# GLU contraction in two parts around the S5 steps of a hybrid decoder trunk, and a chunk's gelu and split one step behind its state

## The chip, the cores and the metric

The kernel runs on one core of one Trainium2 chip. The metric is the device time of one execution in microseconds; the time before is 2535.65 us, the median of three runs (2535.18 to 2535.86). A TensorE clock of 1.0 in the tables is 2.4 GHz, 0.5 is 1.2 GHz.

## The reference

One inference step of a trunk with two layers, each followed by a SwiGLU feed-forward network (FFN) with 5632 hidden channels. The first layer is an even one (retention beside a gated recurrence, after one projection), the second an odd one:

```
u = rmsnorm(x, g)
h_t = A h_{t-1} + B u_t          # S5: 128 groups of 16 channels, 64 complex states each
y_t = Re(C h_t) + d * u_t
y = gelu(y)
z = y @ w_glu + b_glu            # 2048 x 4096
z1, z2 = split(z, 2)
x = x + z1 * sigmoid(z2)
x = x + swiglu(rmsnorm(x, g2))
```

The tokens are a prompt of 256 and 8 samples of 4; the kernel holds them as 288 columns, 72 (8 samples and 64 chunks of the prompt) for each of 4 positions. All is float32.

## The kernel before

**Matmuls.** A product in float32 is made of three in a shorter type: a high part of the weights (`wh`) times the high and the low part of the operand, and the low part (`wl`) times the high part (lines 314 to 316). A *unit* makes one output tile of 128 channels; one *k* is 128 input channels, so 3 matmuls of 288 columns. GLU has 16 k and 32 units, z and g for each of 16 output tiles.

**Weights.** They come in *slots* of half a unit, 8 k for GLU. For each slot SyncE loads `raw` (line 262, 4 buffers), ScalarE copies it to `wh` (line 268, 4 buffers), and VectorE subtracts to get `wl` (line 274, through the helper at L96). The `wl` buffers are a list, `ring`: three, and a fourth, `wlx`, that `to_ffn0` adds for all that follows the first layer's mixer. A buffer returns to the free list when the last matmul of its slot has been issued in program order; the next `wl` takes the oldest free one.

**Order.** All engines' queues are written out by hand in one pass of `run_prog` over a list of items (a unit's half, or a function). Ahead of every item, a function too, the loop at lines 294 to 303 loads and splits ahead of the slots used up:

```
while c[1] < min(c[0], done + LH + 1, n):
    prep_next()
if c[2] >= done + (4 if hold else 3) or c[2] >= n or c[2] in hold:
    break
prepl_next()
```

So `wl` is kept three slots ahead; while `hold` is set (the S5 steps but the last), four, and not the slot named in it.

**S5.** `s5_open` (in the background queue near the end of FFN0) opens the buffers and loads the first tables. `s5_core` computes the norm and then runs 16 steps, one for each chunk of 128 channels (8 groups). `stage_a(j)` issues loads of tables P, R, T and O for the next steps, then P of chunk j+1 (`st_a`: a VectorE multiply by the norm, then 32 narrow matmuls into `pp`, L1396), the first half of chunk j's recurrence on VectorE (`st_b1`: two products, a sum), and T of chunk j (`st_t`: 32 narrow matmuls into `po`, L1446). `stage_b(j)` issues O of chunk j-1 (`st_o`: 64 narrow matmuls that need the state `Hs` of chunk j-1, L1456) and the second half of chunk j (`st_b2`: two scans, two products, and their difference, the state `Hs`). Gelu and split of a chunk follow two to four steps behind: `st_d1` (three ScalarE operations), `st_d1b` (a product, tanh), `st_d2` (VectorE, ScalarE), `st_d3` (VectorE).

**GLU beside S5.** Between `stage_a(t)` and `stage_b(t)`, from t = 4, stand the matmuls of one k, t-4, of the first two units, over the full 16 k; four more stages after the steps (t = 16 to 19) end them, and a third unit runs in a bank of its own. The other 29 units follow, each over all 16 k at once.

Of the kernel before, what the change touches and what calls it, by code (L numbers as in the profile page):

```python
# [46 lines left out]
def trunk_kernel(ctx: ExitStack, tc: tile.TileContext, ins, outs, upto=99, dbg=None):  # L47
# [6 lines left out]
    xgp = ctx.enter_context(tc.tile_pool(name="xgp", bufs=32))  # L54
# [16 lines left out]
    def xg_(dt=F32R):  # L71
        return xgp.tile([P, N], dt, tag="x", name=nm("xg"))

# [144 lines left out]
    def run_prog():  # L218
        ws, items, hold, fin_h = [], [], [], set()
        own = None  # L220
        lead = [u for u in prog if isinstance(u, Unit)][:4]
        for u in prog:
            if isinstance(u, Unit):
                if u in lead[1:]:
                    continue
                hs = [halves_of(x) for x in (lead if u is lead[0] else (u,))]
                for e in range(2):
                    for h in hs:
                        items.append((len(ws),) + h[e])
                        ws.append(h[e])  # L230
            elif isinstance(u, tuple):
                us, stages = u
                hs = [halves_of(x) for x in us]
                idx = {}
                for x, e in ((0, 0), (1, 0), (0, 1), (1, 1), (2, 0), (2, 1)):
                    idx[x, e] = len(ws)
                    ws.append(hs[x][e])
                items.append(lambda h=idx[2, 0]: hold.append(h))
                own = us[2]
                for a, segs, b, free in stages:  # L240
                    items.append(a)
                    for x, k0, k1 in segs:
                        items.append((idx[x, k0 >= hs[x][0][2]], us[x], k0, k1))
                    items.append(b)
                    if free:
                        items.append(hold.clear)
            else:
                items.append(u)
# [6 lines left out]

        def size(i):
            return (ws[i][2] - ws[i][1]) * P

        def dma(i):
            u, a, b = ws[i]  # L260
            r = wt.tile([P, 1024], F32, tag="raw", name=nm("raw"), bufs=RAW)
            sp.dma_start(r[:, :size(i)], u.w[:, a * P:b * P])
            raws[i] = r

        def prep_h(i):
            w = size(i)
# [4 lines left out]
        def prep_l(i):  # L271
            w = size(i)
# [20 lines left out]
        for h in items:  # L293
            while True:
# [4 lines left out]
                if c[2] >= done + (4 if hold else 3) or c[2] >= n or c[2] in hold:  # L299
                    break  # L300
# [4 lines left out]
            i, u, a, b = h  # L305
            if a == u.k0:
                bank = mp_() if u in lead else S["bank"]() if u is own else psa.tile([P, 512], F32, tag="acc", name=nm("acc"))
                accs[id(u)] = (bank[:, :N], u.rhs())
            acc, rhs = accs[id(u)]
            wh, wl, w0 = whs[i], wls[i], ws[i][1]  # L310
# [11 lines left out]
            if b == ws[i][2]:  # L322
                whs.pop(i)
                free.append(wls.pop(i))
                fin_h.add(i)
                while done in fin_h:
                    done += 1
# [7 lines left out]
    def start(dma_next, prep_h, prep_l):  # L335
# [21 lines left out]
        def xl(j):  # L357
            l = xg_()
# [495 lines left out]
    def final_hook(gcol, accbox, lstname, alloc_l=None):  # L854
# [108 lines left out]
    def to_ffn0():  # L963
# [370 lines left out]
    def s5_open():  # L1334
# [22 lines left out]
        for k, j in (("P", 0), ("P", 1), ("R", 0), ("T", 0)):  # L1357
            load(k, j)

    def s5_core():  # L1360
# [40 lines left out]
        def st_b1(j):  # L1401
# [8 lines left out]
            st_d3(j - 4)  # L1410
# [5 lines left out]
        def st_b2(j):  # L1416
# [16 lines left out]
            tabs.pop(("p", j))  # L1433

# [40 lines left out]
        def st_d2(j):  # L1475
            y, s, t_ = tabs.pop(("y", j))
            stt(s, t_, 1.0, y, ADD, MUL)
            h, l = ac_(), xg_()
# [4 lines left out]
        def st_d3(j):  # L1483
            if j < 0:
                return
# [5 lines left out]
        def stage_a(j):  # L1491
            load("P", j + 2)
            load("R", j + 1)
            load("T", j + 1)
            load("O", j)
            if 0 <= j - 2 < NT:
                st_d1(j - 2)
            if j + 1 < NT:
                st_a(j + 1)
            if j >= NT:  # L1500
                st_d3(j - 4)
# [4 lines left out]
        def stage_b(j):  # L1506
            if 0 <= j - 1 < NT:
                st_o(j - 1)
            if j < NT:
                st_b2(j)  # L1510
            else:
                if 0 <= j - 2 < NT:
                    st_d1b(j - 2)
                if 0 <= j - 3 < NT:
                    st_d2(j - 3)
            if j == NT + 3:
                s5_end()
        S["a"], S["b"] = stage_a, stage_b
        S["bank"] = lambda: ps5.tile([P, 2, 512], F32, tag="p", name=nm("pp"))[:, 0]
# [26 lines left out]
    def glu():  # L1546
        us = []
        fin = final_hook(V_FFN1, {}, "xg", lambda: S["x2"].tile([P, N], F32R, tag="x", name=nm("x2")))
        for j in range(NT):
            st = {}  # L1550

            def e1(ps, j=j, st=st):
                z = g_()
                ts(z, ps, vec[:, V_BG + j:V_BG + j + 1], None, ADD)
                st["z"] = z

            def e2(ps, j=j, st=st):
                t_ = g_()
                act.activation(t_, ps, AF.Tanh, scale=0.5, bias=hb2[:, j:j + 1])
                stt(t_, t_, 1.0, st["z"], ADD, MUL)  # L1560
                stt(X[:, j, :], t_, 0.5, X[:, j, :], MUL, ADD)
                later(max(7 - 2 * j, 0), lambda: fin(j))
            us.append(Unit(ins["w_glu"][j], 0, NT, lambda: xs["y"], e1))
            us.append(Unit(ins["w_glu"][NT + j], 0, NT, lambda: xs["y"], e2))
        stages = []
        for t in range(NT + 4):
            segs = [(x, t - 4, t - 3) for x in range(2) if t >= 4]
            if t == NT + 1:
# [170 lines left out]
```

## Time and profile before

| | |
|---|---|
| median of three runs | 2535.65 us |
| profiled execution: span from first to last instruction | 2533.9 us |
| median of the runs less this span | 1.75 us |
| TensorE busy | 2468.4 us, 97% |
| VectorE busy | 1592.1 us, 63% |
| ScalarE busy | 1152.4 us, 45% |
| HBM read | 423.99 MB, 184 GB/s over the span with what is written |

The profiled execution's time outside its span is not on the page; the 1.75 us stand for it. Matmuls are pipelined, so a matmul's listed time (about 295 ns at 288 columns) is over twice the distance from one to the next, which is what counts. The even mixer runs to about 550 us of the span, FFN0 with the tables for S5 to 1366, the S5 steps to 1476, GLU to 1675, then FFN1 and the last norm.

### The profile page before, as it was taken

How to read it: one execution, taken by the hardware profiler on the slowest of the kernel's cores; microseconds unless marked ns; L12 is line 12 of the kernel's file. 1: busy time of each engine (PE TensorE's matmuls, PEld its weight loads, DVE VectorE, ACT ScalarE, POOL GpSimd, SP SyncE). 2: the span in 40 equal slices, each digit the busy share in tenths (PEclk: the TensorE clock that was granted, in tenths of full speed). 3: DMA queues.
4: the chain of work that ended last, by engine and by line, in shares of the span. 5: the costliest groups of instructions: out<-in, count | busy, mean ns of one | idle time of the engine just before them, and what ended most of it. 6: DMA issues, size and time to landing. Idle time of an engine off the chain costs nothing.

```text
span 2533.9 us, 49270 instructions
## 1 busy us (share of the span) xinstructions
PE 2468.4 (97%) x20210; PEld 2428.2 (96%) x20210; DVE 1592.1 (63%) x2955; ACT 1152.4 (45%) x1786; POOL 104.7 (4%) x204
## 2 busy tenths in 40 slices
PE   8999999999999999999998789999999999999997
PEld 8899999999999999999997689999999999999997
DVE  7767666567766777667756975555544555445555
ACT  6646545433455655545533344443333333333342
POOL 0111110000000000000100000000000000000000
PEclk9999999999999999999999999999999999999999
DMA  7556645555566666666678855555455554445553
GB/s 251 181 173 193 203 151 181 164 166 167 182 217 198 209 199 207 212 210 196 204 239 250 277 163 165 167 164 166 164 163 173 166 164 161 161 163 166 167 163 125
DMA packets 155184, 468.31 MB, mean 185 GB/s; under 512 B 32912, under 2 KB 40976, under 8 KB 154960
## 3 DMA queue, kind: packets, MB, share of 16 engines
q1 hardware_dynamic: 140944, 421.16, 51.9%
q0 software_dynamic: 12288, 42.69, 4.6%
q8 instruction: 159, 2.61, 0.4%
q10 hardware_dynamic: 1728, 1.33, 0.2%
q14 instruction: 65, 0.53, 0.1%
HBM read 423.99 MB, written 41.11 MB: 184 GB/s over the span
## 4 chain that ended last, share of the span: by engine, by line
PE 92%; DVE 5%; DMA 2%; ACT 1%; issue 0%; SPq 0%; POOL 0%; DVEq 0%; ACTq 0%
PE acc L314 30%; PE acc L316 29%; PE acc L315 29%; DVE w L96 2%; DVE w L1421 1%; DMA raw<-in_w_in_dram 1%; PE mp L724 1%; PE mp L1244 1%; PE mp L776 0%; DVE Hs L96 0%; DVE g L105 0%; PE mp L1261 0%; PE mp L519 0%; DVE g L96 0%; DMA tab<-tabR 0%
## 5 line engine op out<-in xcount | busy, mean ns | idle before, releaser
L314 PE MATMUL acc<-xg,wh 128*128 128x288 f32 x3520 | 1047.9, 298 | 0.0
L268 ACT ACTIVATE wh<-raw 128x1024 fp32r<-128x1024 f32 (+1 forms) x736 | 758.9, 1035 | 426.2 <-PE acc L315 277.2
L316 PE MATMUL acc<-xg,wl 128*128 128x288 f32 x2816 | 829.0, 294 | 0.8 <-DVE wl L96 0.8
L315 PE MATMUL acc<-xg,wh 128*128 128x288 f32 x2608 | 765.5, 294 | 1.6 <-DVE xg L105 1.6
L96 DVE TENSOR_TENSOR wl<-raw,wh 128x1024 fp32r<-128x1024 f32 (+1 forms) x585 | 692.2, 1196 | 56.2 <-ACT wh L268 48.5
L314 PEld LDWEIGHTS acc<-xg,wh 128*128 128x128 f32 x3520 | 660.5, 188 | 3.0 <-issue 2.2
L314 PE MATMUL acc<-ac,wh 128*128 128x288 f32 x2064 | 613.5, 297 | 1.6 <-ACT ac L1479 1.0
L316 PEld LDWEIGHTS acc<-xg,wl 128*128 128x128 f32 x2816 | 529.2, 188 | 1.1 <-DVE wl L96 1.1
L315 PEld LDWEIGHTS acc<-xg,wh 128*128 128x128 f32 x2608 | 492.3, 189 | 2.5 <-DVE xg L105 2.0
L316 PE MATMUL acc<-ac,wl 128*128 128x288 f32 x1592 | 469.5, 295 | 0.7 <-DVE wl L96 0.7
L315 PE MATMUL acc<-ac,wh 128*128 128x288 f32 x1568 | 460.1, 293 | 0.0
L315 PE MATMUL acc<-x,wh 128*128 128x288 f32 x1408 | 415.4, 295 | 0.0
L314 PEld LDWEIGHTS acc<-ac,wh 128*128 128x128 f32 x2064 | 388.6, 188 | 4.7 <-issue 1.7
L96 DVE TENSOR_TENSOR g<-acc,rstd 128x288 f32<-128x288 f32 x192 | 87.6, 456 | 353.0 <-PE acc L316 352.5
L316 PEld LDWEIGHTS acc<-ac,wl 128*128 128x128 f32 x1592 | 300.0, 188 | 1.2 <-DVE wl L96 1.2
L315 PEld LDWEIGHTS acc<-ac,wh 128*128 128x128 f32 x1568 | 295.5, 188 | 0.0
L315 PEld LDWEIGHTS acc<-x,wh 128*128 128x128 f32 x1408 | 264.4, 188 | 0.1
L316 PE MATMUL acc<-xg,wlx 128*128 128x288 f32 x704 | 207.3, 294 | 0.0
L96 DVE TENSOR_TENSOR X<-X,acc 128x288 f32<-128x288 f32 x112 | 50.8, 454 | 243.2 <-PE acc L316 242.9
L96 DVE TENSOR_TENSOR wlx<-raw,wh 128x1024 fp32r<-128x1024 f32 (+1 forms) x151 | 179.4, 1188 | 6.8 <-ACT wh L268 6.8
L191 ACT ACTIVATE ac<-g 128x288 fp32r<-128x288 f32 x98 | 43.5, 444 | 286.9 <-DVE g L96 286.9
L316 PE MATMUL acc<-ac,wlx 128*128 128x288 f32 x472 | 139.2, 295 | 0.0
(279 smaller groups left out, 2030.3 us busy)
## 6 DMA issues: line engine op xcount, KB each, us to landing
raw<-in_w_gu_dram SPq DMA_DIRECT2D x352, 512.0 KB, 4.5
raw<-in_w_dn_dram SPq DMA_DIRECT2D x128, 448.0 KB, 4.1
raw<-in_w_in_dram SPq DMA_DIRECT2D x96, 512.0 KB, 4.5
raw<-in_w_dn_dram SPq DMA_DIRECT2D x64, 512.0 KB, 3.7
raw<-in_w_glu_dram SPq DMA_DIRECT2D x64, 512.0 KB, 4.7
raw<-in_w_out_dram SPq DMA_DIRECT2D x32, 512.0 KB, 4.4
out_ret_s_dram<-s POOLq DMA_DIRECT2D x16, 512.0 KB, 4.9
tabR<-R POOLq DMA_DIRECT2D x16, 512.0 KB, 6.8
```

The source lines that it names most:

```text
L96: v.tensor_tensor(o, a, b, op=op)
L191: act.activation(h, x, AF.Copy, scale=scale)
L268: act.activation(wh[:, :w], raws[i][:, :w], AF.Copy)
L314: pe.matmul(acc, lhsT=wh[:, o:o + P], rhs=xh, start=(k == u.k0), stop=False)
L315: pe.matmul(acc, lhsT=wh[:, o:o + P], rhs=xl, start=False, stop=False)
L316: pe.matmul(acc, lhsT=wl[:, o:o + P], rhs=xh, start=False, stop=(k == u.k1 - 1))
L724: pe.matmul(CR[h][32 * g:32 * g + 32, :256], lhsT=qm[:, dt, b2, :], rhs=t_[:, b2, dt, :], start=(c < 2 and dt == 0), stop=(c > 1 and dt == 1),
L1244: pe.transpose(ps[:, (2 * k + ri) * P:(2 * k + ri + 1) * P], st["ps"][:, ri, 4 * (jj // 2) + q].rearrange("p s i -> p (s i)"), ident)
L1421: v.tensor_tensor_scan(g[:, ri].rearrange("p q c -> p (q c)"), r4m, a[:, ri].rearrange("p q c -> p (q c)"), 0.0, op0=MUL, op1=ADD)
```

## The change

GLU's 16 k are cut at 4. For 30 of the 32 units (all z, and g of output tiles 0 to 13) a *first part* over k 0 to 3 runs as a unit of its own; ScalarE copies its bank to an SBUF tile. Two first parts share a slot. The first two run one k a step in steps 2 to 5; from step 5 on each step holds two whole first parts (three in steps 7, 10, 13), and three are left behind the last step. Second parts over k 4 to 15 run afterwards in order, in slots of 6 k, and add the kept tile when they leave their bank; g of tiles 14 and 15 has all 16 k there.

O of the chunk before moves to the head of a step (ahead of the next P), and its gelu and split run in the same step: `st_d1` right behind O, `st_d1b`, `st_d2` and `st_d3` in `st_b2`. R and O of a first chunk more are loaded in `s5_open`, and a step's loads are issued as R, O, T, P. The norm's matmul writes its sums for the 4 positions to 4 partition groups, so that one add follows it. The fourth `wl` buffer is gone, and so is `hold`: `wl` is three slots ahead throughout. The 32 tiles `xg` become 16 for high parts and kept z parts, and 16 (`xl`) for low parts.

```diff
-    xgp = ctx.enter_context(tc.tile_pool(name="xgp", bufs=32))
+    xgp = ctx.enter_context(tc.tile_pool(name="xgp", bufs=16))
...
-                if c[2] >= done + (4 if hold else 3) or c[2] >= n or c[2] in hold:
+                if c[2] >= done + 3 or c[2] >= n:
...
-            if b == ws[i][2]:
+            left[i] -= b - a
+            if left[i] == 0:
                 whs.pop(i)
                 free.append(wls.pop(i))
...
-        t_ = AP_["st"].enter_context(tc.tile_pool(name="wt2", bufs=1)).tile([P, 1024], F32R, name="wlx")
-        S["ring"].append(t_)
-        S["free"].append(t_)
...
-        for k, j in (("P", 0), ("P", 1), ("R", 0), ("T", 0)):
+        for k, j in (("P", 0), ("P", 1), ("R", 0), ("T", 0), ("R", 1), ("O", 0)):
             load(k, j)
...
-        pe.matmul(ps, lhsT=ones, rhs=S["acc"], start=True, stop=True)
+        for s in range(CH):
+            pe.matmul(ps[32 * s:32 * s + 32, :NC], lhsT=ones[:, :32], rhs=S["acc"][:, s * NC:s * NC + NC], start=True, stop=True,
+                      tile_position=(0, 32 * s), skip_group_check=True)
...
-        for s in range(CH):
-            ts(m4[32 * s:32 * s + 32], ps[32 * s:32 * s + 32, s * NC:s * NC + NC], 1.0 / D, EPS, MUL, ADD)
+        ts(m4, ps[:, :NC], 1.0 / D, EPS, MUL, ADD)
...
-            st_d3(j - 4)
...
-            if j >= 2:
-                st_d1b(j - 2)
+            if j >= 1:
+                st_d1b(j - 1)
             tt(a, g, cos, MUL)
             tt(b, g[:, ::-1], sin, MUL)
-            if j >= 3:
-                st_d2(j - 3)
+            if j >= 1:
+                st_d2(j - 1)
...
+            if j >= 1:
+                st_d3(j - 1)
...
         def stage_a(j):
+            if j:
+                load("R", j + 1)
+                load("O", j)
+            load("T", j + 1)
             load("P", j + 2)
-            load("R", j + 1)
-            load("T", j + 1)
-            load("O", j)
-            if 0 <= j - 2 < NT:
-                st_d1(j - 2)
+            if j >= 1:
+                st_o(j - 1)
+                st_d1(j - 1)
...
         def stage_b(j):
-            if 0 <= j - 1 < NT:
-                st_o(j - 1)
...
+        KS = 4
...
+        def first(key, w, alloc):
+            def ev(ps):
+                part[key] = alloc()
+                act.activation(part[key], ps, AF.Copy)
+            return Unit(w, 0, KS, lambda: xs["y"], ev)
+
+        g1 = [first(("g", j), ins["w_glu"][NT + j], lambda: ac_(F32)) for j in range(NT - 2)]
+        g1 += [first(("z", j), ins["w_glu"][j], lambda: xg_(F32)) for j in range(NT)]
+        slots = [[(u, 0, KS) for u in g1[2 * i:2 * i + 2]] for i in range(NT - 1)]
+        todo = deque(g1[2:])
+        seq = []
+        for t in range(NT + 1):
+            seq.append(lambda t=t: S["a"](t))
+            if 2 <= t < KS + 2:
+                seq += [(u, t - 2, t - 1) for u in g1[:2]]
+            if t > KS:
+                n = len(todo) if t == NT else 3 if t % 3 == 1 else 2
+                m = n if t < NT else 0
+                seq += [(todo.popleft(), 0, KS) for _ in range(m)]
+            seq.append(lambda t=t: S["b"](t))
+        seq += [(u, 0, KS) for u in todo]
+        prog.append((slots, seq))
...
+                stt(z, ps, vec[:, V_BG + j:V_BG + j + 1], part.pop(("z", j)), ADD, ADD)
...
+                if ("g", j) in part:
+                    src = t_
+                    tt(t_, ps, part.pop(("g", j)), ADD)
```

## Rows read from the trace of the kernel before

**Rows 1.** The page, busy time of each engine (share, instructions).
```profile
PE 2468.4 (97%) x20210; PEld 2428.2 (96%) x20210; DVE 1592.1 (63%) x2955; ACT 1152.4 (45%) x1786; POOL 104.7 (4%) x204
```

**Rows 2.** Stretches: length, PE, PEld, DVE, ACT, POOL busy; clock, DMA, GB/s.
```profile
1380.00:1480.00 100.00, 71.05 (x2040) 60.98 (x2038) 95.37 (x177) 38.20 (x107) 7.64 (x16) 0.89 0.80 258
...
1520.00:1600.00 80.00, 80.00 (x607) 80.00 (x606) 41.69 (x56) 33.45 (x44) 0.00 (x0) 1.00 0.53 170
```

**Rows 3.** Waits of TensorE, 1376 to 1476: total us, times, longest.
```profile
PE pp L1396 <- ACT g L1463: 18.8, 10, 2.4
```

**Rows 4.** One step in time, VectorE: start, us, operation, idle before it.
```profile
1431.32 0.45 DVE L96 TENSOR_TENSOR xg<-xg,r4n 128x288 f32<-128x288 f32 x1
...
1433.97 1.28 DVE L1421 TENSOR_TENSOR_SCAN w<-tab,w 128x256 f32<-128x256 f32 x2
...
1437.08 0.69 DVE L96 TENSOR_TENSOR Hs<-w,w 128x512 f32<-128x512 f32 x1
```

**Rows 5.** In time: end of two GLU pairs, and FFN1's first matmul line.
```profile
1599.93 0.46 DVE L105 SCALAR_TENSOR_TENSOR X<-g,X 128x288 f32<-128x288 f32 x1
...
1625.32 0.46 DVE L105 SCALAR_TENSOR_TENSOR X<-g,X 128x288 f32<-128x288 f32 x1
...
1674.81 0.29 PE L314 MATMUL acc<-xg,wh 128*128 128x288 f32 x1
```

**Rows 6.** Even mixer in time: first matmuls of two halves, and wl.
```profile
402.68 0.30 PE L314 MATMUL acc<-ac,wh 128*128 128x288 f32 x1
...
405.86 0.29 PE L314 MATMUL acc<-ac,wh 128*128 128x288 f32 x1
...
406.11 1.23 DVE L96 TENSOR_TENSOR wl<-raw,wh 128x1024 fp32r<-128x1024 f32 x1 [0.52 <-issue]
```

**Rows 7.** One step in time: P, T, first GLU matmul, O, bank's copy, P.
```profile
1425.50 1.22 PE L1396 MATMUL pp<-xg,tab 128*64 128x72 f32 x32 [0.88 <-ACT g L1463]
...
1426.65 0.71 PE L1446 MATMUL po<-xg,T 128*32 128x72 f32 x32
...
1427.29 0.40 PE L314 MATMUL acc<-ac,wh 128*128 128x288 f32 x1
...
1428.29 1.23 PE L1456 MATMUL po<-Hs,tab 128*32 128x72 f32 x64
...
1431.18 0.39 ACT L1463 ACTIVATE g<-po 128x288 f32<-128x288 f32 x1
...
1431.87 1.22 PE L1396 MATMUL pp<-xg,tab 128*64 128x72 f32 x32 [2.36 <-ACT g L1463]
```

**Rows 8.** VectorE in time: norm, wlx, H(0), wait for R(1), H(4), H(15).
```profile
1367.82 0.95 DVE L102 TENSOR_SCALAR g<-po 32x72 f32<-32x72 f32 x4
...
1372.05 1.22 DVE L96 TENSOR_TENSOR wlx<-raw,wh 128x1024 fp32r<-128x1024 f32 x1
...
1378.35 0.69 DVE L96 TENSOR_TENSOR Hs<-w,w 128x512 f32<-128x512 f32 x1
...
1382.10 1.29 DVE L96 TENSOR_TENSOR w<-pp,tab 128x512 f32<-128x512 f32 x2 [2.69 <-DMA tab<-tabR]
...
1405.25 0.68 DVE L96 TENSOR_TENSOR Hs<-w,w 128x512 f32<-128x512 f32 x1
...
1474.90 0.68 DVE L96 TENSOR_TENSOR Hs<-w,w 128x512 f32<-128x512 f32 x1
```

**Rows 9.** TensorE in time: a P at the lower clock.
```profile
1379.51 2.19 PE L1396 MATMUL pp<-xg,tab 128*64 128x72 f32 x32 [2.79 <-DVE xg L96]
```

**Rows 10.** Stretches behind the opening of S5.
```profile
1270.00:1275.00 5.00, 5.00 (x40) 5.00 (x39) 0.00 (x0) 0.00 (x0) 0.00 (x0) 1.00 1.04 332
1275.00:1280.00 5.00, 3.77 (x27) 3.30 (x26) 2.28 (x4) 1.90 (x2) 0.00 (x0) 1.00 0.69 223
```

**Rows 11.** Waits of TensorE, whole run: for wl.
```profile
PE acc L316 <- DVE wl L96: 1.6, 3, 0.8
```

More of the change, by code (lines that the diff above doesn't have):

```diff
@@ L72, in xg_, with xl_ @@
         return xgp.tile([P, N], dt, tag="x", name=nm("xg"))
+    def xl_():
+        return xgp.tile([P, N], F32R, tag="xl", name=nm("xl"))
     def ac_(dt=F32R, w=N):
@@ L218, in run_prog, with slot @@
     def run_prog():
-        ws, items, hold, fin_h = [], [], [], set()
-        own = None
+        ws, items, where, left = [], [], {}, []
+        def slot(*pieces):
+            o = 0
+            for u, a, b in pieces:
+                for k in range(a, b):
+                    where[id(u), k] = (len(ws), a - o)
+                o += b - a
+            ws.append(pieces)
+            left.append(o)
         lead = [u for u in prog if isinstance(u, Unit)][:4]
@@ L228, in run_prog @@
                     for h in hs:
-                        items.append((len(ws),) + h[e])
-                        ws.append(h[e])
+                        items.append(h[e])
+                        slot(h[e])
             elif isinstance(u, tuple):
[L232 to L246, printed above, removed]
+                for pieces in u[0]:
+                    slot(*pieces)
+                items.extend(u[1])
             else:
@@ L304, in run_prog @@
                 continue
-            i, u, a, b = h
+            u, a, b = h
+            i, w0 = where[id(u), a]
             if a == u.k0:
-                bank = mp_() if u in lead else S["bank"]() if u is own else psa.tile([P, 512], F32, tag="acc", name=nm("acc"))
+                bank = mp_() if u in lead else psa.tile([P, 512], F32, tag="acc", name=nm("acc"))
                 accs[id(u)] = (bank[:, :N], u.rhs())
             acc, rhs = accs[id(u)]
-            wh, wl, w0 = whs[i], wls[i], ws[i][1]
+            wh, wl = whs[i], wls[i]
             for k in range(a, b):
@@ L321, in run_prog @@
                     u.evac(acc)
-            if b == ws[i][2]:
+            left[i] -= b - a
+            if left[i] == 0:
                 whs.pop(i)
                 free.append(wls.pop(i))
-                fin_h.add(i)
-                while done in fin_h:
-                    done += 1
+                assert i == done
+                done += 1
                 step[0] += 1
@@ L1511, in stage_b @@
             else:
[L1512 to L1516, printed above, removed]
+                st_d1b(j - 1)
+                st_d2(j - 1)
+                st_d3(j - 1)
                 s5_end()
         S["a"], S["b"] = stage_a, stage_b
-        S["bank"] = lambda: ps5.tile([P, 2, 512], F32, tag="p", name=nm("pp"))[:, 0]
         def s5_end():
@@ L1546, in glu @@
     def glu():
-        us = []
+        KS = 4
         fin = final_hook(V_FFN1, {}, "xg", lambda: S["x2"].tile([P, N], F32R, tag="x", name=nm("x2")))
-        for j in range(NT):
-            st = {}
[L1552 to L1557, printed above, removed]
-                t_ = g_()
-                act.activation(t_, ps, AF.Tanh, scale=0.5, bias=hb2[:, j:j + 1])
+        part = {}
@@ L1561, in e2 @@
                 stt(X[:, j, :], t_, 0.5, X[:, j, :], MUL, ADD)
[L1562 to L1568, printed above, removed]
-                segs.append((2, 0, 8))
-            if t == NT + 3:
-                segs.append((2, 8, 16))
-            stages.append((lambda t=t: S["a"](t), segs, lambda t=t: S["b"](t), t == NT - 1))
@@ L1573, in glu @@
-        prog.append((us[:3], stages))
-        prog.extend(us[3:])
+                later(max(3 - j, 0), lambda: fin(j))
+            unit(ins["w_glu"][j], KS, NT, lambda: xs["y"][KS:], e1)
+            k0 = KS if j < NT - 2 else 0
+            unit(ins["w_glu"][NT + j], k0, NT, lambda: xs["y"][k0:], e2)
+        for j in range(NT):
+            pair(j)
     def dump(name):
```

29 lines of the change are left out of this document (16 added, 13 removed).

## The prediction

> **What bounds the kernel now.** The page comes first: TensorE is busy 2468.4 of 2533.9 us [rows 1]. So only time in which TensorE stands still can be won, and the reader is to look for where that is. The table by stretches answers it: from 1380 to 1480, the S5 steps, TensorE is busy 71.05 of 100 us, VectorE 95.37, and the granted clock averages 0.89 [rows 2]. In the waits of TensorE there, the S5 input matmuls (P) wait 18.8 us in ten steps [rows 3]; the release is put down to ScalarE, but each P starts 0.1 us after the VectorE multiply that makes its operand. One step in order of time [rows 4] shows VectorE going from one operation to the next for 6.3 us without a gap, from the multiply (1431.32) to the state H (1437.77). Here VectorE is the bound and TensorE waits for it; everywhere else TensorE is the bound.
>
> **What the change moves.** Before, 72 GLU matmuls run in steps 0 to 15 (steps 4 to 15, two tiles, one k, three matmuls each). After, tiles 0 and 1 take 24 there, and steps 5 to 15 hold 25 tiles of 12 matmuls: 324. The other three first parts and all second parts follow. That is 252 matmuls fewer behind the last state. Two GLU pairs, 192 matmuls, take 1625.32 - 1599.93 = 25.39 us [rows 5], 0.1322 us each: 33.3 us leave the stretch behind H(15).
>
> **What it adds: weights have to be split inside the steps.** Each half-tile slot (24 matmuls) needs a ScalarE copy and a VectorE subtraction wl. Before, a fourth wl buffer let four slots be made ready ahead, and none was made in the steps up to H(14). After, three buffers are left, and each of the 13 slots that end in steps 5 to 15 puts one wl into VectorE's queue, ahead of that step's second half (scans, rotation, H). If a wl cost only its 1.2 us, this would be 15.6 us.
>
> **Which buffer wl writes** decides what it costs. With three buffers and three slots ahead, the only free one is that of the slot whose matmuls were issued just before. So wl must wait until TensorE has done them. The even mixer, which runs on three buffers, shows this: a half starts on TensorE at 402.68, the next half at 405.86; VectorE, idle for 0.52 us, starts wl at 406.11 [rows 6]. There it costs nothing, as nothing urgent is behind it. In an S5 step everything is behind it, and the slot stands on TensorE behind the output matmuls O of the step before, which the change puts first in the step and which need the previous H. So a loop closes: H, O, P, T, slot, wl, scans, next H. VectorE's first half (multiply to sum) hides in its wait.
>
> One turn, from rows: H to O 0.1 (as multiply to P); O 1.15 (1.23 long, and groups of this length let the next start 0.07 early, as P with 1.22 does after 1.15); P 1.15; T 0.64 [rows 7]; slot 24 x 0.1322 = 3.17; wl starts 0.25 after the next matmul could [rows 6]; wl 1.2; from first scan to the end of H 1437.77 - 1433.97 = 3.80 [rows 4]. Sum 11.46. Where a slot ends after the first tile of a step (steps 8, 9, 14, 15) it is 12 matmuls, 1.58 less: 9.88. Step 5 ends the slot of tiles 0 and 1 (6 matmuls, 0.79) and one whole slot: 12.25. Step 10 has three tiles and two slot ends, 1.59 more than the ordinary step: 13.05. Steps 6, 7, 11, 12, 13 are ordinary. Together 5 x 11.46 + 4 x 9.88 + 12.25 + 13.05 = 122.1 us. Before, H(4) to H(15) is 1475.58 - 1405.93 = 69.65 [rows 8]. **Added: 52.4 us.** Bounds of this term: 15.6 (wl hidden from TensorE, rival 1) and 52.4 plus the clock term below.
>
> **The start.** One 128-partition add replaces four of 0.95 us together, and the fourth wl (1.22) leaves the place ahead of the first products [rows 8]; P of chunk 0 is then last, so of these 1.9 us I take 0.9 (bounds 0.7 and 1.9). Rotation table 1 is loaded earlier, so the 2.69 us that VectorE waited for it [rows 8] go; but gelu and split now sit in step 1 already. H(0) at 1379.04 - 0.9 = 1378.1, four steps of 6.33 (69.65 / 11): H(4) at 1403.4 instead of 1405.93. **Gain 2.5.** P's table is now issued last of a step's loads, behind four T loads; in steps 1 to 4 it may land 1 to 2 us late, which TensorE can hide there (no slot yet); in steps of 11 us it is early. SyncE's queue also gets a weight load behind each wl, whose raw buffer it reuses, with the next step's tables behind it; the first of these (R) waits for the scans after that wl anyway, and the others have a whole turn: 0.
>
> **The end.** From H(15), 1475.58, to FFN1's first matmul at 1674.8 [rows 5] there are 199.2 us; 1464 matmuls are 193.5; the 5.7 left are O, waits for the last chunks' gelu, and some slow clock. After, the three first parts left over cover the gelu of chunk 15; O and about 2 us of the rest stay: **gain 2.5** (bounds 0 and 4.5).
>
> **The clock.** From 1380 to 1480 the granted clock is 0.89 on average [rows 2], that is some 22% of the time at 1.2 instead of 2.4 GHz, and a P there takes 2.19 instead of 1.22 us [rows 9]. Before, this hid behind VectorE. After, TensorE's part of each turn is on the path, 122.1 - 11 x 5.0 = 67 us; at 0.89 it takes 8.3 more, and the pauses are longer (about 5 us a turn instead of 2.4). Lower bound 0; upper bound O, P and T of each of the 11 turns at half clock, 11 x 2.94 = 32.3. I take **9**, near the row of this stretch.
>
> By the Trainium skill, page TensorE: Matmul & The Clock Gate, section "HAM oscillation", a kernel whose matmul bursts are parted by waits begins each burst at the low clock. By that rule the term would be the upper bound. The trace before agrees only in part: with a pause in each step most bursts still ran fast.
>
> **The loads.** When S5 opens, SyncE issues state and tables, then the next weights; TensorE stands still for 1.2 us of 1275 to 1280, and 332 GB/s move from 1270 to 1275 [rows 10]. Two more tables of 0.52 MB now go ahead of the weights: 1.05 MB at 332 GB/s, **3.2 us** more standstill (bounds 0, if they share the queues without pushing, and 5).
>
> **Taken at nothing.** The 30 ScalarE copies of first parts (0.39 each, as the copy of O's bank [rows 7]) lie in a stretch where ScalarE is busy 38 of 100 us [rows 2], in its wait for VectorE; uncovered they are 12 us. The 14 adds and the second operand of 16 sums lie in the GLU, where TensorE runs without a gap and VectorE is busy 41.69 of 80 us [rows 2]; uncovered some 6. Three instead of four buffers in both FFNs: the whole run, the even mixer with three included, shows TensorE waiting 1.6 us for wl [rows 11]; I take 0, bounds 0 and 5. FFN0 is where VectorE also builds the tables, so the first place to look.
>
> **Sum.** -2.5 + 52.4 - 33.3 - 2.5 = 14.1; + 9 + 3.2 = 26.3 us on the span of 2533.9: 2560.2. The median of the runs shown lies 1.75 above this span: **2562 us**.
>
> **Rivals.**
> 1. *A wl costs only itself*, and the steps stay VectorE's at 6.33: H(15) at 1403.4 + 69.65 + 13 x 1.2 = 1488.7, 13.1 later than before, for 33.3 + 2.5 moved: -22.7 + 3.2 = -19.5, so 2516 us, faster. For it: VectorE has no gap before, and TensorE's total work a step (6 to 8 us) would fit beside 7.5. It decides if the slot is done before VectorE comes to wl, about 2.6 us after H; the slot's end is at 4.9 at the earliest. Chance 0.14.
> 2. *Every burst begins at half clock*: 14.1 + 32.3 + 3.2 = 49.6, so 2585 us. For it: the pauses double; against: the row of 0.89. Chance 0.13.
> 3. *The loop is there, but a turn is about 2.4 us shorter*, since wl or the scans find their operands earlier than I have it; all cancels, 2536 us. No row speaks for it but the sum's own uncertainty. Chance 0.06.
>
> My forecast has 0.67; its own range is 2545 to 2578 (clock 0 to 18, loads 0 to 5, turns within 0.7 us). The range 2538 to 2586 leaves out rival 1 and the tails of the others. Within 0.2% (5 us) a measurement of this kernel can't tell a difference from none. Faster: rival 1 and little of rival 3, 0.15; same: most of rival 3, 0.05; slower: 0.80.
>
> **What would show it.** Right: wl waiting for the third GLU matmul line, 13 times and 2 to 4 us each; O waiting for Hs some 5 us in each of steps 6 to 15; H spaced 10 to 13 us from step 5 on and 6.3 before; VectorE well under 95% there; H(15) near 1537. Wrong: H spaced 7 to 8 us with VectorE still full (rival 1), or P and T at twice their time in each step (rival 2). The standstill near 1277 grows to 4 us if the loads' term holds; wl waits of TensorE at 730 to 1250 would show the lost fourth buffer.

## The result and the profile after

The changed kernel takes 2578.42 us, the median of four runs (2573.74 to 2579.82), against 2535.76 for the kernel before beside it (2535.18 to 2537.29): a ratio of 1.0167, 95% interval 1.0155 to 1.0180. The forecast was 2562, in a range of 2538 to 2586. The profiled execution took 2579.82 us with a span of 2577.4, so it lies 1.4 us above the median; on the spans the change costs 43.5 us where 26.3 were forecast. Slower, as said, and by more than said.

The page's busy times, the line that answers to [rows 1]:

```profile
PE 2488.8 (97%) x20216; PEld 2447.5 (95%) x20216; DVE 1609.6 (62%) x2981; ACT 1167.4 (45%) x1831; POOL 104.0 (4%) x204
```

TensorE is busy 20.4 us longer with nearly the same instructions, which is what a slower clock and a slower pace look like. Two stretches, the S5 steps and the GLU behind them, with the columns of [rows 2]:

```profile
1410.00:1540.00 130.00, 87.27 (x1557) 80.18 (x1554) 76.56 (x131) 44.34 (x104) 3.58 (x10) 0.80 0.58 179
1560.00:1700.00 140.00, 139.67 (x1049) 139.63 (x1049) 93.08 (x149) 66.76 (x104) 0.54 (x1) 1.00 0.56 167
```

VectorE has fallen from 95% of the S5 stretch to 59%, TensorE is busy 67%, and the granted clock averages 0.80 where it was 0.89. No engine is full: something goes round in a circle. The waits of VectorE, and then those of TensorE, from 1370 to 1560 (columns of [rows 3]):

```profile
DVE wl L99 <- PE acc L316: 56.5, 13, 7.1
```

```profile
PE po L1455 <- ACT ac L1478: 28.5, 9, 5.1
PE po L1455 <- DVE Hs L99: 23.2, 7, 5.1
```

VectorE waits for TensorE (13 times, for the third GLU matmul line), and TensorE waits for VectorE (16 times, O for the state H). The first of TensorE's two lines names ScalarE, but each of its O starts within 0.1 us of the end of a `Hs`, as the next rows show. One whole turn, step 6: first VectorE, then TensorE, in time (start, us, operation, idle before it and what ended it).

```profile
1426.93 0.69 DVE L99 TENSOR_TENSOR Hs<-w,w 128x512 f32<-128x512 f32 x1
...
1429.59 0.69 DVE L99 TENSOR_TENSOR w<-w,w 128x512 f32<-128x512 f32 x1
1435.98 1.23 DVE L99 TENSOR_TENSOR wl<-raw,wh 128x1024 fp32r<-128x1024 f32 x1 [5.70 <-PE acc L316]
1437.12 1.27 DVE L1418 TENSOR_TENSOR_SCAN w<-tab,w 128x256 f32<-128x256 f32 x2
...
1440.23 0.69 DVE L99 TENSOR_TENSOR Hs<-w,w 128x512 f32<-128x512 f32 x1
```

```profile
1427.67 2.15 PE L1455 MATMUL po<-Hs,tab 128*32 128x72 f32 x64 [5.08 <-DVE Hs L99]
1429.75 2.16 PE L1394 MATMUL pp<-xg,tab 128*64 128x72 f32 x32
1431.84 0.71 PE L1445 MATMUL po<-xg,T 128*32 128x72 f32 x32
...
1441.01 2.15 PE L1455 MATMUL po<-Hs,tab 128*32 128x72 f32 x64 [5.07 <-ACT ac L1478]
```

The reader is to follow H (ends 1427.62), O (1427.67), P, T, two GLU tiles, wl (1435.98, after 5.70 us of idle VectorE), scans, H (ends 1440.92), O (1441.01). And to see that O and P take 2.15 and 2.16 us, twice their time, while T at 0.71 is back at full clock.

The markers of [rows 8] and [rows 5] after the change (VectorE: H(0), H(4), H(15); then TensorE: FFN1's first matmul):

```profile
1386.85 0.69 DVE L99 TENSOR_TENSOR Hs<-w,w 128x512 f32<-128x512 f32 x1
...
1412.73 0.69 DVE L99 TENSOR_TENSOR Hs<-w,w 128x512 f32<-128x512 f32 x1
...
1554.61 0.68 DVE L99 TENSOR_TENSOR Hs<-w,w 128x512 f32<-128x512 f32 x1
```

```profile
1718.56 0.30 PE L314 MATMUL acc<-xg,wh 128*128 128x288 f32 x1
```

From such markers the 43.5 us come apart; times in us, ends of H taken as start plus length, "norm" the first matmul of the norm of S5 and "transpose" the last of the 128-column transposes in FFN0.

| stretch | before | after | difference | forecast |
|---|---|---|---|---|
| start to last transpose (1247.1, 1252.7) | 1247.1 | 1252.7 | +5.6 | 0 |
| transpose to norm | 119.8 | 123.7 | +3.8 | +3.2 |
| norm to H(0) to H(4) | 39.0 | 37.1 | -1.9 | -2.5 |
| H(4) to H(15) | 69.65 | 141.88 | +72.2 | +61.4 (loop 52.4, clock 9) |
| H(15) to FFN1's first matmul | 199.2 | 163.3 | -36.0 | -35.8 |
| FFN1's first matmul to the end | 859.1 | 858.8 | -0.3 | 0 |

Two rows are off: the steps by 10.8 us, and a stretch by 5.6 us for which no term stood.

### The profile page after: what moved, and what is told of

Its sections match the earlier page's. It is cut to its first block, busy times and chain, and to the rows that moved or that the text cites. A ratio compares the mean times of both kernels' runs of the same rounds, so it can differ in the third digit from the quotient of the medians.

```text
span 2577.4 us, 49550 instructions
## 1 busy us (share of the span) xinstructions
PE 2488.8 (97%) x20216; PEld 2447.5 (95%) x20216; DVE 1609.6 (62%) x2981; ACT 1167.4 (45%) x1831; POOL 104.0 (4%) x204
## 4 chain that ended last, share of the span: by engine, by line
PE 94%; DVE 4%; DMA 1%; ACT 1%; issue 0%; SPq 0%; DVEq 0%; ACTq 0%
PE acc L314 29%; PE acc L316 29%; PE acc L315 29%; DVE w L99 1%; PE po L1455 1%; PE pp L1394 1%; DVE wl L99 1%; DVE w L1418 1%; PE mp L724 1%; PE mp L1241 1%; DVE g L108 0%; DMA raw<-in_w_in_dram 0%; PE po L1445 0%; PE mp L776 0%; PE mp L1258 0%
## 5 line engine op out<-in xcount | busy, mean ns | idle before, releaser
L314 PE MATMUL acc<-xg,wh 128*128 128x288 f32 x3520 | 1047.8, 298 | 0.0
L99 DVE TENSOR_TENSOR wl<-raw,wh 128x1024 fp32r<-128x1024 f32 (+2 forms) x751 | 877.4, 1176 | 265.9 <-issue 162.4
L316 PE MATMUL acc<-xg,wl 128*128 128x288 f32 x3520 | 1035.2, 294 | 0.9 <-DVE wl L99 0.9
L267 ACT ACTIVATE wh<-raw 128x1024 fp32r<-128x1024 f32 (+2 forms) x751 | 762.3, 1019 | 406.9 <-PE acc L315 248.7
L315 PE MATMUL acc<-xl,wh 128*128 128x288 f32 x2624 | 774.9, 295 | 0.0
L316 PEld LDWEIGHTS acc<-xg,wl 128*128 128x128 f32 x3520 | 662.9, 188 | 1.2 <-DVE wl L99 1.2
L314 PEld LDWEIGHTS acc<-xg,wh 128*128 128x128 f32 x3520 | 659.7, 187 | 3.0 <-issue 2.0
L316 PE MATMUL acc<-ac,wl 128*128 128x288 f32 x2080 | 614.5, 295 | 0.3 <-DVE wl L99 0.3
L315 PEld LDWEIGHTS acc<-xl,wh 128*128 128x128 f32 x2624 | 494.0, 188 | 0.5
L316 PEld LDWEIGHTS acc<-ac,wl 128*128 128x128 f32 x2080 | 392.8, 189 | 0.6 <-DVE wl L99 0.6
L108 DVE SCALAR_TENSOR_TENSOR g<-g,g 128x288 f32<-128x288 f32 (+3 forms) x187 | 75.2, 402 | 19.1 <-ACT g L1579 14.3
L1455 PE MATMUL po<-Hs,tab 128*32 128x72 f32 x1024 | 28.9, 289 | 51.7 <-ACT ac L1478 28.5
```

The lines of the kernel that those rows point to most:

```text
L99: v.tensor_tensor(o, a, b, op=op)
L108: v.scalar_tensor_tensor(o, a, s, b, op0=op0, op1=op1)
L267: act.activation(wh[:, :w], raws[i][:, :w], AF.Copy)
L314: pe.matmul(acc, lhsT=wh[:, o:o + P], rhs=xh, start=(k == u.k0), stop=False)
L315: pe.matmul(acc, lhsT=wh[:, o:o + P], rhs=xl, start=False, stop=False)
L316: pe.matmul(acc, lhsT=wl[:, o:o + P], rhs=xh, start=False, stop=(k == u.k1 - 1))
```

## Experiments

**1. Weights split ahead of a step's tiles, not behind them.** The theory: a loop closes because wl is queued ahead of the scans and waits for the GLU tiles of its own step. If so, moving the same wl ahead of the next step's tiles (where its buffer has been free for long) opens it. What then sets the step was open: VectorE alone, or a second loop over ScalarE, since tanh (needed by VectorE's last product ahead of H) stands in ScalarE's queue behind the copies of first parts, which also wait for the step's tiles. The edit lets a weight slot be made ready only at the first GLU item of a step (`late` holds the step's other items):

```diff
...
-            while True:
+            while h not in late:
...
+            s0 = len(seq)
             seq.append(lambda t=t: S["a"](t))
...
+            ab += [x for x in seq[s0:] if x is not seq[s0 + 1]]
...
```

> The changed kernel, but within the S5 steps the weight work (load, wh, wl) of a slot used up in a step is put into the queues of the next step, ahead of its first GLU tile, instead of ahead of the step's second half. So wl no longer waits for the slot just issued. Theory A (two loops: wl behind the slot on VectorE, and behind it, hidden so far, tanh of st_d1b on ScalarE behind the copies of the first parts, which wait for TensorE too, with st_d2 and H behind that tanh): a turn is 8.4 us with two tiles and 10.0 with three, H(4) to H(15) 98 us at full clock, some 103 measured, against 141.9; time near 2539 us. Theory B (wl's wait is the only loop): VectorE's own work sets the steps, 11 x 6.37 + 13 x 1.15 = 85 us from H(4) to H(15), time near 2522. Theory C (the added time is in wl's own work and the clock, not in the wait): no change, 2574 to 2580.

The kernel before, run beside this and the other experiments, took 2534.4 to 2534.9 us, and all ratios are to it. Measured: 2549.8 us, ratio 1.0059 (1.0041 to 1.0077); H(4) to H(15) 109.02 instead of 141.88. VectorE's largest wait from 1376 to 1560, and a step in time, ScalarE and then VectorE:

```profile
DVE g L108 <- ACT g L1472: 22.9, 9, 4.5
```

```profile
1441.37 0.41 ACT L1547 ACTIVATE ac<-acc 128x288 f32<-128x288 f32 x1 [1.90 <-PE acc L317]
1442.96 0.41 ACT L1547 ACTIVATE ac<-acc 128x288 f32<-128x288 f32 x1 [1.18 <-PE acc L317]
1444.55 0.41 ACT L1547 ACTIVATE ac<-acc 128x288 f32<-128x288 f32 x1 [1.18 <-PE acc L317]
1444.86 0.43 ACT L1472 ACTIVATE g<-g 128x288 f32<-128x288 f32 x1
```

```profile
1445.33 0.46 DVE L108 SCALAR_TENSOR_TENSOR g<-g,g 128x288 f32<-128x288 f32 x1 [3.94 <-ACT g L1472]
1445.70 0.68 DVE L99 TENSOR_TENSOR Hs<-w,w 128x512 f32<-128x512 f32 x1
```

The wait of wl for TensorE is gone and 32.9 us with it: the first loop is shown. A second one stands behind it, as theory A had it, though the steps take 6 us and the kernel some 11 more than it gave: three copies wait for three tiles, tanh (L1472) for the copies, the gelu product for tanh, H for the product.

**2. Tanh ahead of the copies as well.** In addition to the edit of 1, `st_d1b(j - 1)` moves from `st_b2` to the end of `stage_a`, ahead of the step's tiles.

```diff
-            if j >= 1:
-                st_d1b(j - 1)
...
+            if j >= 1:
+                st_d1b(j - 1)
...
```

> As the kernel with the weight work in the next step, and st_d1b (product and tanh) at the end of stage_a, so ahead of the copies of the first parts on ScalarE. Theory A: both loops are gone, H(4) to H(15) is 85 to 92 us (VectorE full, three-tile steps a little longer), time 2522 to 2530. Theory B: the same as without the tanh moved, within 2 us.

Measured: 2538.65 us, eight runs (2534.16 to 2542.35), ratio 1.0017 (1.0006 to 1.0027); H(4) to H(15) 100.17, more than expected. Five steps come down to 7.8 to 8.0 us, but three stay long (H(5) to H(6) 11.06, H(7) to H(8) 14.89, H(10) to H(11) 10.36; the last two stand behind the steps with three tiles). The longest, on VectorE and then on ScalarE in time:

```profile
1438.23 0.69 DVE L99 TENSOR_TENSOR Hs<-w,w 128x512 f32<-128x512 f32 x1
1446.07 0.46 DVE L108 SCALAR_TENSOR_TENSOR xl<-g,ac 128x288 fp32r<-128x288 f32 x1 [7.15 <-ACT ac L1477]
```

```profile
1445.29 0.41 ACT L1546 ACTIVATE ac<-acc 128x288 f32<-128x288 f32 x1 [1.18 <-PE acc L317]
1445.60 0.44 ACT L1477 ACTIVATE ac<-g 128x288 fp32r<-128x288 f32 x1
```

A third loop of the same kind: the split's low part (`xl`) waits for its high part (`ac`, L1477), which ScalarE runs behind the copies of that step's tiles (the third of them above); the next step's first VectorE operations wait behind `xl`. The tiles of that step were late themselves, as T stopped for 2.89 us without a wait that the trace shows (more on such stops in experiment 4).

**3. The clock held, too much.** The theory on the missing 10.8 us: the pauses of 3.4 to 5.1 us drop the clock, and the O and P that follow, on the loop's path, run at 1.2 GHz. So fill the pause with float32 matmuls of 224 columns into spare columns of a PSUM bank, which nothing reads. Here 34 of them in each of steps 5 to 15, into the bank of O and T, which also changes part of the S5 sums.

```diff
...
         def stage_b(j):
+            if 5 <= j < NT:
+                for _ in range(34):
+                    pe.matmul(S["po"][:, N:], lhsT=ones, rhs=X[:, 0, :512 - N], start=True, stop=True, skip_group_check=True)
```

> The changed kernel with 34 idle matmuls of 224 columns (0.1 us each at full clock) behind the GLU tiles of steps 5 to 15, into unused columns of a bank, so that TensorE does not pause while it waits for the next state; nothing else is changed. Theory A (the 20 us by which steps 5 to 15 exceed 122 are O, P and the first matmuls at half clock): granted clock near 1 from step 6 on, O and P at 1.2 instead of 2.2 us, H(4) to H(15) 122 us, time 2556 to 2560. Rival (the excess is in other waits, and the clock only shows it): H(4) to H(15) stays at 140 or grows by what the idle matmuls push O back.

Measured: 2653.19 us, ratio 1.0467 (1.0448 to 1.0486). One such matmul took 0.39 us, not 0.1 (the trace has two instructions for each), so 13 us were put into a pause of 5: most steps took 19.1 to 19.2 us, and from 1420 to 1620 TensorE never stood still. It says nothing of the clock's price.

**4. The clock held, to measure.** The same with 9 matmuls (3.5 us) into the spare columns of P's bank.

```diff
...
+            if 5 <= j < NT:
+                for _ in range(9):
+                    pe.matmul(S["pp"][:, 0, N:], lhsT=ones, rhs=X[:, 0, :512 - N], start=True, stop=True, skip_group_check=True)
```

> The changed kernel with 9 idle matmuls of 224 columns (0.39 us each at full clock, by the run with 34 of them) behind the GLU tiles of steps 5 to 15, into unused columns of a bank that nothing accumulates in, 3.5 us that lie in TensorE's wait for the next state. Theory A (the 20 us by which steps 5 to 15 exceed 122 are matmuls at half clock): O and P take 1.2 instead of 2.2 us, H(4) to H(15) is 120 to 126 us, time 2556 to 2563. Rival (the excess is in other waits): 138 us or more, time 2573 or more.

Measured: 2567.02 us, ratio 1.0128 (1.0110 to 1.0147): with more work, 11.4 us less than the changed kernel. The clock of the steps (columns of [rows 2]), then O, P and T of step 7 on TensorE:

```profile
1411.00:1555.00 144.00, 127.98 (x2034) 120.14 (x2033) 95.53 (x162) 56.48 (x130) 5.40 (x14) 0.99 0.56 172
```

```profile
1435.77 1.22 PE L1455 MATMUL po<-Hs,tab 128*32 128x72 f32 x64 [1.67 <-ACT ac L1478]
1436.92 1.22 PE L1394 MATMUL pp<-xg,tab 128*64 128x72 f32 x32
1438.07 0.71 PE L1445 MATMUL po<-xg,T 128*32 128x72 f32 x32
...
1462.85 0.44 PE L1445 MATMUL po<-xg,T 128*32 128x72 f32 x12 [2.92 <-issue]
...
1501.11 0.69 PE L1445 MATMUL po<-xg,T 128*32 128x72 f32 x26 [3.38 <-issue]
```

H(4) to H(15) is 129.14, 3 us above what theory A gave, so 12.7 us of the 141.88 went with the clock. The steps one by one (us from H to H) show more than the sum:

| step | 5 | 6 | 7 | 8 | 9 | 10 | 11 | 12 | 13 | 14 | 15 | sum |
|---|---|---|---|---|---|---|---|---|---|---|---|---|
| forecast at full clock | 12.25 | 11.46 | 11.46 | 9.88 | 9.88 | 13.05 | 11.46 | 11.46 | 11.46 | 9.88 | 9.88 | 122.1 |
| after | 14.20 | 13.29 | 14.67 | 11.39 | 12.38 | 14.71 | 14.04 | 13.90 | 13.83 | 9.82 | 9.66 | 141.9 |
| clock held | 12.90 | 11.41 | 11.46 | 9.82 | 13.10 | 13.11 | 11.83 | 16.68 | 11.47 | 9.83 | 7.53 | 129.1 |

Held, six of eleven steps are within 0.07 us of the sum made from rows of before. Two are long for another reason: steps 9 and 12 hold the two stops of 2.92 and 3.38 us inside T for which the trace shows no wait (the rows above); behind the second, the step's 24 GLU matmuls took 4.8 us (1501.73 to 1506.54) instead of 3.2. Their excess over the forecast, 3.2 and 5.2, more than makes up the 7.0 between 129.1 and 122.1. Step 15 is 2.35 short, and not by the clock: it has no P (1.15 in the sum), and its wl splits 6 k and not 8, took 0.96 us and started behind 6 of the tile's 12 matmuls.

**5. The fourth wl buffer given back.** The change took it out; with it, the next wl need not go into the buffer of the slot just issued. In addition to the changed kernel, in `to_ffn0`:

```diff
+        t_ = AP_["st"].enter_context(tc.tile_pool(name="wt2", bufs=1)).tile([P, 1024], F32R, name="wlx")
+        S["ring"].append(t_)
+        S["free"].append(t_)
```

> The changed kernel with the fourth wl buffer given back after the first mixer, as before the change; wl is still kept three slots ahead, so it now writes the buffer of a slot that ended one slot earlier. Theory A (wl's wait goes, but the copies of the first parts and wh, which still has four buffers, hold up tanh on ScalarE until the slot is done): H(4) to H(15) is 104 us at full clock, some 110 measured, time near 2546. Theory B (the lost buffer was all of it): near 87 us, time near 2523. Theory C (buffers are not the cause): 140 us, 2574 or more.

Measured: 2551.74 us, ratio 1.0068 (1.0050 to 1.0086); H(4) to H(15) 116.63. VectorE's two largest waits from 1376 to 1560:

```profile
DVE g L108 <- ACT g L1474: 24.8, 10, 4.3
DVE wl L99 <- ACT wh L267: 7.1, 2, 4.1
```

One buffer of 0.5 MB is worth 26.7 us (2578.42 - 2551.74), 25.2 of them in the steps: wl no longer waits for TensorE, and tanh is late in its place, 10 times, as in experiment 1. That is theory A, with the time some 6 us above what it gave. So the loop is a loop over that buffer, by two edits that have nothing in common.

**6. The 5.6 us before S5: how the tiles lie in SBUF.** No wait answers to them, and they grow only where the moving operands are high and low parts of the group `xg`: 1.2 us late at 403 of the span and still at 498 (the operand is `ac`), 2.8 at 697 and still at 788, 4.4 at 996. The prediction's place to look was the lost wl buffer, but the changed kernel also makes 32 tiles `xg` into 16 and 16. So: the kernel before, with its four buffers, and only this changed.

```diff
-    xgp = ctx.enter_context(tc.tile_pool(name="xgp", bufs=32))
+    xgp = ctx.enter_context(tc.tile_pool(name="xgp", bufs=16))
...
+    def xl_():
+        return xgp.tile([P, N], F32R, tag="xl", name=nm("xl"))
...
-            l = xg_()
+            l = xl_()
...
```

> The kernel before with one part of the change alone: the 32 tiles xg become 16 for high and 16 for low parts, with everything else as before. The changed kernel was 5.9 us late when FFN0 ended, spread evenly over the stretches whose moving operands are xg and xl, with no wait listed. Theory A (the place of these tiles): FFN0's end is 4 to 6 us later than before and the time is 2540 to 2542. Rival (three instead of four wl buffers): no difference, 2535 to 2537.

And the same two groups of 16, each tile under a name of its own so that high and low parts alternate in SBUF:

```diff
...
-        return xgp.tile([P, N], dt, tag="x", name=nm("xg"))
+        xc[0] += 1
+        return xgp.tile([P, N], dt, tag=f"x{xc[0] % 16}", name=nm("xg"))
+
+    def xl_():
+        xc[1] += 1
+        return xgp.tile([P, N], F32R, tag=f"l{xc[1] % 16}", name=nm("xl"))
...
```

> The kernel before with 16 tiles for high and 16 for low parts, as in the run with two tags, but laid out in SBUF in turn (high 0, low 0, high 1, low 1, ...), as the 32 tiles of the kernel before lay. Theory A (the 6.2 us of the run with two tags come from the addresses): no difference from before, 2533 to 2537. Rival (from which buffer is reused when, and so from waits): 2540 to 2542 again.

Measured: two blocks 2540.85 (2539.26 to 2541.89, ratio 1.0023, 1.0013 to 1.0032), alternating 2527.41 (2524.99 to 2527.93, ratio 0.9970, 0.9959 to 0.9982), where no change had been expected. The last group of transposes on TensorE, of the kernel before, of the two blocks, of the alternating tiles:

```profile
1246.75 0.60 PE L1244 MATMUL mp<-ident,pst 128*128 128x128 f32 x4
```

```profile
1251.93 0.60 PE L1247 MATMUL mp<-ident,pst 128*128 128x128 f32 x4
```

```profile
1247.21 0.60 PE L1251 MATMUL mp<-ident,pst 128*128 128x128 f32 x4
```

So 5.2 of the 5.6 us are the two blocks' alone. From FFN1's first to its last matmul on a low part (tile `x`; 1674.93 to 2429.06 before, 1673.48 to 2420.13 alternating) it is 754.1 and 746.7. The same instructions run at another pace. The mean distance from one matmul to the next where the operands are such high and low parts (distances across records missing from the trace left out):

| | FFN0 | FFN1 |
|---|---|---|
| before | 132.2 ns | 133.3 ns |
| two blocks, and after the change | 133.3 ns | 133.3 ns |
| alternating | 132.4 ns | 131.7 ns |

Where the moving operand is `ac`, a group that no edit touched, it is 132.2 to 132.3 ns in FFN0 and 132.1 to 132.6 in FFN1.

One pattern fits all six entries. By their code, FFN0's high parts are handed out in turn with low parts in the kernel before and in the alternating one, and in a row with two blocks; FFN1's, whose low parts have a pool of their own in every kernel (`x2`), are in turn with other tiles in the alternating kernel alone. In a row goes with 133.3 ns, in turn with 131.7 to 132.4. The addresses themselves are in no trace, and no run was made to test the pattern.

**7. The same repair in the changed kernel**, nothing else.

> The changed kernel with one edit: the tiles for high and low parts laid out in turn. Theory (the layout costs by itself, as in the kernel before): the end of FFN0's tables at 1247 instead of 1252.7, some 12 us less in all, 2564 to 2569. Rival (the layout is worth something only where TensorE never waits, so not here): 2574 or more.

Measured: 2566.58 us (2565.20 to 2568.99), ratio 1.0124 (1.0109 to 1.0140), inside what was expected; last transpose at 1247.4, 747 us between the same two matmuls of FFN1. H(4) to H(15) stays at 141.77: layout and loop are two things.

**8. The loads.** R of chunk 1 and O of chunk 0 loaded where `s5_core` starts rather than in `s5_open`, in the changed kernel.

```diff
-        for k, j in (("P", 0), ("P", 1), ("R", 0), ("T", 0), ("R", 1), ("O", 0)):
+        for k, j in (("P", 0), ("P", 1), ("R", 0), ("T", 0)):
...
+        S["load"]("R", 1)
+        S["load"]("O", 0)
```

> The changed kernel with one edit: tables R and O of the first chunks are loaded at the head of s5_core and not ahead of the weights in s5_open. Theory (the two tables push the weights back, and TensorE stands still for 3 to 4 us more near 1281, some of it then at half clock): from the last table transpose to the norm 118 to 120 instead of 123.7 us, time 4 us less, 2571 to 2576. Rival (the tables share the queues without cost): 123 to 124 us, no change.

Measured: 2576.48 us (2575.36 and 2577.60), ratio 1.0165 (1.0147 to 1.0184). The stretches that answer to [rows 10], first of the changed kernel, then of this one, and a wait of TensorE in the latter, in time:

```profile
1280.00:1285.00 5.00, 2.90 (x23) 2.67 (x21) 0.03 (x1) 0.95 (x1) 0.00 (x0) 1.00 1.03 400
1285.00:1290.00 5.00, 4.72 (x18) 4.37 (x19) 4.46 (x7) 3.07 (x4) 0.00 (x0) 0.50 0.35 114
```

```profile
1280.00:1285.00 5.00, 5.00 (x40) 5.00 (x39) 3.24 (x6) 3.35 (x5) 0.00 (x0) 1.00 0.84 295
1285.00:1290.00 5.00, 4.99 (x38) 4.76 (x37) 3.96 (x5) 2.86 (x4) 0.00 (x0) 1.00 0.67 223
```

```profile
1386.99 2.19 PE L1396 MATMUL pp<-xg,tab 128*64 128x72 f32 x32 [2.93 <-DMA tab<-tabR]
```

The standstill goes (transpose to norm 118.2 instead of 123.7, 5.5 less), and with it the half clock behind it (0.50 in the second stretch of the changed kernel, 1.00 here; its matmuls were 0.24 us apart from 1285.0 to 1291.6). But R(1) is then late again, as it was before the change: H(0) to H(4) is 28.5 instead of 25.9. Half is given back, and the rest is within what two runs can tell.

**9. What these point to.** Experiment 2 with the alternating tiles and the later loads:

> The changed kernel with the weight work in the next step and tanh early (2538.7 us), with the tiles for high and low parts laid out in turn, and with tables R and O of the first chunks loaded at the head of s5_core instead of ahead of the weights in s5_open. Theory (the parts add up): 6.2 less for the layout, 2 to 4 less for the loads: 2528 to 2531, faster than before. Rival (the loads only move, and the layout costs nothing beside this order): 2535 to 2540.

Measured: 2527.35 us (2523.23 to 2528.18), ratio 0.9970 (0.9958 to 0.9982), a little under what was expected. The alternating tiles alone in the kernel before give 2527.41, so the schedule, its two loops opened, is worth nothing yet. H(4) to H(15) is 102.89; the third loop is still in it, with a wait of 9.1 us in one step. Then `st_d2` and `st_d3` moved one more step back and ahead of the tiles' copies:

```diff
...
+            if j >= 2:
+                st_d2(j - 2)
             if j >= 1:
                 st_o(j - 1)
...
+            if j >= 2:
+                st_d3(j - 2)
...
```

> The kernel of the run that put the parts together (2527.4 us), with the second half of gelu and the split of a chunk (st_d2, st_d3) one step later and ahead of the copies of the first parts in ScalarE's queue, so that no operation of VectorE in a step waits for TensorE's GLU tiles. Theory (ScalarE's copies behind the tiles are the last loop; there VectorE waited 11 us in five steps for the split's high part): H(4) to H(15) goes from 103 to 86 to 92 us, time 2510 to 2518. Rival (TensorE's own pauses set these steps): no change, 2524 to 2529.

Measured: 2520.86 us (2519.43 to 2523.11), ratio 0.9946 (0.9933 to 0.9958): faster than both kernels, a little above the time expected. H(4) to H(15) is 94.80 (86 to 92 were expected), with six of the last seven steps at 7.83 to 7.84. VectorE's largest waits and then TensorE's from 1376 to 1560:

```profile
DVE g L103 <- ACT g L1465: 9.5, 8, 3.2
DVE g L103 <- PE acc L321: 6.9, 5, 1.4
DVE xl L112 <- ACT ac L1479: 3.4, 4, 2.2
```

```profile
PE po L1456 <- issue: 11.2, 5, 3.0
PE po L1456 <- DVE Hs L103: 7.1, 3, 2.9
PE pp L1401 <- DMA tab<-tabR: 4.5, 1, 4.5
```

VectorE's waits are spread thin now. The first line of TensorE names no cause, but each of its five O starts 0.10 to 0.11 us behind the end of a `Hs`, as every O that waits for the state does; in step 6, VectorE and then TensorE:

```profile
1425.19 0.69 DVE L103 TENSOR_TENSOR Hs<-w,w 128x512 f32<-128x512 f32 x1
```

```profile
1425.98 2.15 PE L1456 MATMUL po<-Hs,tab 128*32 128x72 f32 x64 [2.85 <-issue]
```

So what is left on TensorE is the wait for the state, the late table, and one stop of 1.90 us inside T. Against the alternating tiles in the kernel before, the schedule now gains about 6.5 us (2527.41 - 2520.86): moving 33 us of matmuls pays when the splits, tanh and the gelu's copies all stand ahead of the tiles, and not before.

## Why the prediction was right, and where not

**The loop (52.4 us): right, to 0.1 us in six of eleven steps.** The wait of wl for the third GLU line is there 13 times, and each O starts on H. With the clock held, ordinary steps without a stop (6, 7, 13) are 11.41 to 11.47 against 11.46, short ones (8, 14) 9.82 and 9.83 against 9.88 and the one with three tiles 13.11 against 13.05. Step 15 was reckoned wrong: the sum has a P there, and a wl of full size, and is 2.35 us too long. The waits were put at 2 to 4 us; they are 4.3 on average (56.5 / 13), because the slow O and P lie in them: with the clock held, those of steps 6, 7 and 13 are 3.8 to 3.9 instead of 5.7 to 7.1. Rival 1 (a wl costs only itself) is out: steps of 6.5 us end at step 5, the first with a split. But the loop named was one of three through the same GLU tiles. The other two, over ScalarE, lay hidden behind it; "30 ScalarE copies at nothing" held only as long as wl was later than they were.

**The clock (9 us): the step of the sum that failed, a size and not a mechanism.** After less forecast, step by step in the table above, is 19.8 us. The clock's part can be read off the rows directly: O takes 2.12 to 2.15 us instead of 1.22 in nine of steps 5 to 15, P 1.84 to 2.19 in nine, and T about 1.2 instead of 0.71 in six, 19.3 us together. Slow GLU matmuls and a stop of 0.93 us in T of step 7 add some 2.9, which the 2.35 of step 15 nearly hide: without that luck the miss would look larger than 10.8. In step 6 O and P give 0.93 + 0.94 = 1.87, and that step is 1.83 over the forecast; in step 14, where both ran fast after a pause of 3.44 us, it is 0.06 under. The prediction took the mean clock of a stretch in which TensorE had paused 1.9 us on average and 2.4 at most ahead of P [rows 2, 3], and in which 7 of 10 P (1406 to 1465) took 1.22 to 1.28 us, and let it stand for one in which the pauses of steps 6 to 15 are 3.4 to 5.1. With the clock that came, its own way of reckoning gives 67 x (1 / 0.80 - 1) = 16.8. Holding the clock gave back 12.7 us; the remaining 7 went to the two unexplained stops and what followed them, less step 15.

Rival 2 (every burst at half clock, 32.3) was nearer on this term than the forecast on some steps and further on the sum: O pays nearly always, P mostly, T in half of the steps, together 60% of its price (19.3 of 32.3). The Trainium skill, page TensorE: Matmul & The Clock Gate, section "HAM oscillation — how this bites in real kernels", has each burst behind a long wait (there for a DMA) begin at the low clock. The rows of steps 6 to 15 agree in nine of ten: O, first behind the pause, took 2.12 to 2.15 us in all but step 14, where it took 1.23 behind a pause of 3.44 us, as long as the one ahead of the slow O of step 8.

**The stretch before S5 (0): not foreseen.** 5.6 us go here, and 5.2 of them because the moving operands lie elsewhere in SBUF, shown by experiment 6 with nothing else changed. The prediction named "three instead of four buffers in both FFNs" as the thing to watch there; the waits for wl did not grow (1.2 us in the whole run after, 1.6 in [rows 11]), and the last transpose is still at 1252.1 with the fourth buffer given back (experiment 5): the buffers have next to no part in it. Why one layout is about 1% faster than another was not found: which addresses matter was not tried.

**The loads (3.2): 3.8, the size by luck.** That the two tables push the weights back is shown by experiment 8, which takes 5.5 us out. But TensorE's standstill grew by 1.0 us alone (from 0.64 + 0.59 + 0.16 to 2.10 + 0.28), not by 3.2, and its 2.4 us are short of the 4 that were named as the sign. The rest is the half clock behind the stop, which the term did not have.

**Start (-2.5): 1.9 of it came; end and moved matmuls (-2.5, -33.3): right.** The start gave 1.9: H(0) 0.9 earlier from the norm, and 1.0 by H(4), as the first four steps are 6.39 to 6.50, not 6.33. H(15) to FFN1 is 36.0 shorter, forecast 35.8.

Of the 17.2 us between forecast and result, the steps have 10.8 (the clock, less what step 15 hides), the layout 5.6, the loads 0.6 and the start 0.6; the end and FFN1 give back 0.5.

## What to carry to other kernels

When work of one engine is put inside the loop of another, go through each queue of the loop and ask of every instruction ahead of the next state whether it waits for the work put in: here a weight split, a tanh and a gelu's copy did, one hidden behind the other, and only with all three ahead of it did the move pay. A reckoning of such a turn from single durations can be good to a tenth of a microsecond (look once more at the first and the last turn, which may lack a part), but take the duration of whatever follows a longer pause than the trace has seen at the slow clock. Before a difference without a wait is put down to a schedule, look at where operands have moved in SBUF.

## What the runs showed that was not expected

The layout of the moving operands changes the pace of dense matmuls: 131.7 to 133.3 ns from one to the next for the same instructions, and 2540.85, 2534.64 and 2527.41 us for one kernel with its 32 operand tiles in two blocks, in one ring as before, and alternating.

Inside the runs of narrow matmuls there are stops for which no wait is shown: in step 7, ahead of the 28th matmul of T, 0.93 us in the changed kernel and 0.53 to 3.72 in those of experiments 2, 7, 8 and 9, and with the clock held 2.92 in step 9 and 3.38 in step 12. Each ends 1.4 to 1.9 us after a transfer of 16384 bytes on the queue that the trace names "instruction". With the clock held there is a third stop, of 0.26 us among the GLU matmuls of step 11; it and the one of step 12 lie 768 and 1024 of TensorE's instructions behind the one of step 9, 3 and 4 times 256, to within one in the order of records. That points to the loading of instructions in blocks; no run changed it, so it is not shown.
